# The MLP of an encoder layer: way up by Strassen's seven products, sums of the way down kept in DRAM

## The chip, the cores and the metric

The kernel runs on one core of a Trainium2 chip. The metric is device time in microseconds of one execution. The engines are named as in the profile: PE is TensorE's matmul, PEld its weight load, DVE VectorE, ACT ScalarE, POOL GpSimd, SP SyncE. POOL and SP do little but issue DMA transfers here.

## The reference, cut to what matters

Two layers of an encoder over 512 tokens of 1024 channels, all float32. Each has a mixer (three attentions, merged through gates) and an MLP with 4096 hidden channels; the change lies in the MLP.

```
for l in range(DEPTH):                       # DEPTH = 2
    h = _rmsnorm(x, g_mix[l])
    x = x + _mixer(h, ...)                   # ends with merged @ w_out
    h = _rmsnorm(x, g_mlp[l])
    x = x + jnp.square(jax.nn.relu(h @ w_up[l])) @ w_down[l]     # [512,1024] @ [1024,4096], [512,4096] @ [4096,1024]
return _rmsnorm(x, g_final)
```

## The kernel before, in words

Activations are kept transposed, channels on partitions: a chunk is 128 channels by 512 tokens. For precision every operand of a matmul is cut into a high and a low part (both float32r): a copy on ACT makes the high part, a subtraction on DVE the low one. A product is then three matmuls: high by high, high by low, low by high. `wblock` loads 512 KB of weights by a DMA on POOL's queue into a tile `raw` and cuts them into two tiles `w`; `mm3` runs the three matmuls for each of the chunks that it sums over.

**The order.** Nothing runs in the order of the code. `Plan` records all instructions, `schedule` lays them out by a planner's own costs on the five engines, with tiles from a common pool (`T` gives a tile by tag; at most 12 `w` and 6 `raw` live at a time, 8 banks of PSUM), and `emit` writes them out in that order, each engine's as one row. On the chip an engine then takes its instructions strictly in that order and waits by semaphores.

**The MLP.** The hidden channels are 16 pairs of chunks. The way up (`up_pair`) makes two chunks from the eight chunks of `h` by `mm3`: 48 matmuls of 512 columns a pair, then Relu and Square on ACT into a tile `hb`. The norm's factor is left out and multiplied in at the end (R2). The way down is done by Strassen's scheme in Winograd's form: a pair of chunks by two halves of the tokens (HB = 256) is a 2 by 2 block matrix, and so is the weight block, so seven products of 128 x 128 by 128 x 256 stand for eight. The halves' sums (`ht`) and their high and low parts (`u`) are made in `up_pair`, the weights' sums (`ss`) and parts (`w`) in `down_weights`. `PAIRS = (4, 4, 4)`: after each four pairs of the way up, `down` runs for each of the four pairs of output chunks (mp = 0 to 3), 7 x 4 x 3 = 84 matmuls of 256 columns, and `keep` takes the seven sums out of PSUM: copied by ACT into tiles `da` and `db` in the first group, added to them by DVE in the others. The last 4 of the 16 pairs go up and down in the plain way (8 chunks, `mm3`), and `outputs` puts the seven kept sums together on DVE beside that.

Before the MLP stands `wout`: for each of eight output chunks 24 matmuls, an addition to the residual stream `xt` on DVE, and `n2.chunk`, which scales the chunk by the norm's weights, cuts it in two parts (`h`) and sums its squares.

Of the kernel before, what the change touches and what calls it, by code (L numbers as in the profile page):

```python
# [11 lines left out]
F32 = mybir.dt.float32  # L12
# [8 lines left out]
S = 512  # L21
# [23 lines left out]
PAIRS = (4, 4, 4)  # L45
# [55 lines left out]
class Plan:  # L101
# [81 lines left out]
    def record(self, eng, m, args, kw):  # L183
# [8 lines left out]
        for v in outs:  # L192
            if isinstance(v, View):
                writes.append(v)
        for v in ins:
            if isinstance(v, View):
                reads.append(v)
# [416 lines left out]
def trunk(ctx, tc, x, w_in, b_gate, g_mix, diff_lambda, g_diff, g_cq, g_ckv, w_uq, w_ukv,  # L614
# [249 lines left out]
    def layer(l, norm):  # L864
# [714 lines left out]
        n2 = Norm(gmlp)  # L1579
        for mp in range(4):  # L1580
            for i in range(2):
                m = 2 * mp + i
                wh, wl = wblock(w_out[l], 0, 8, 128 * m)
                p = P("mm")
                mm3(p, wh, wl, merged)
                dve.tensor_add(xt[m], xt[m], p)
                n2.chunk(m, xt[m])
            dma(xs[mp], xm[mp])
# [6 lines left out]
        HB = S // 2  # L1595
        sums = {}

        def up_pair(c0):

            b = T("hb", [128, 2, 2, HB])  # L1600
            for i in range(2):
                wh, wl = wblock(w_up[l], 0, 8, c0 + 128 * i)
                p = P("mm")
                mm3(p, wh, wl, h)
                t = T("t")
                act.activation(t, p, AF.Relu)
                act.activation(b[:, i].rearrange("p t n -> p (t n)"), t, AF.Square)
            t13, t24 = T("ht", [128, 2, HB]), T("ht", [128, 2, HB])

            dve.tensor_sub(t13[:, 0], b[:, 0, 1], b[:, 0, 0])  # L1610
            dve.tensor_sub(t13[:, 1], b[:, 1, 1], b[:, 0, 1])
            dve.tensor_sub(t24[:, 0], b[:, 1, 1], t13[:, 0])
            dve.tensor_sub(t24[:, 1], t24[:, 0], b[:, 1, 0])
            parts = []
            for src in (b[:, :, 0], t13, t24):
                u = T("u", [128, 2, 2, HB], F32R)
                copy(u[:, 0], src)
                dve.tensor_sub(u[:, 1], src, u[:, 0])
                parts += [u[:, :, 0], u[:, :, 1]]
            if "u" not in sums:  # L1620
                sums["u"] = T("u", [128, 2, 2, HB], F32R)
                u = sums["u"][:, 0]
            else:
                u = sums.pop("u")[:, 1]
            hilo(u, b[:, 1, 1])
            b11, b21, t1, t3, t2, t4 = parts
            return [b11, b21, u, t4, t1, t2, t3]

        def down_weights(k0, n, mp):

            rows = w_down[l][128 * k0:128 * k0 + 256 * n, 256 * mp:256 * mp + 256].rearrange("(j i p) n -> p i j n", i=2, p=128)
            raw = [load(rows[:, i], n, 256).rearrange("p j (o n) -> p j o n", o=2) for i in range(2)]

            def four(t):
                return t[:, :256 * n].rearrange("p (a j n) -> p a j n", a=2, n=128)
            s12, s34 = four(T("ss", [128, 1024])), four(T("ss", [128, 1024]))

            dve.tensor_add(s12[:, 0], raw[0][:, :, 1], raw[1][:, :, 1])
            dve.tensor_sub(s12[:, 1], s12[:, 0], raw[0][:, :, 0])
            dve.tensor_sub(s34[:, 0], raw[0][:, :, 0], raw[0][:, :, 1])  # L1640
            dve.tensor_sub(s34[:, 1], raw[1][:, :, 0], s12[:, 1])
            wh, wl = pair()
            a1 = [four(w) for w in (wh, wl)]
            for i in range(2):
                copy(a1[0][:, i], raw[i][:, :, 0])
                dve.tensor_sub(a1[1][:, i], raw[i][:, :, 0], a1[0][:, i])
            a2 = four(T("w", [128, 1024], F32R))
            copy(a2[:, 0], raw[1][:, :, 1])
            dve.tensor_sub(a2[:, 1], raw[1][:, :, 1], a2[:, 0])
            ws = []  # L1650
            for s_ in (s12, s34):
                wh, wl = pair()
                copy(four(wh), s_)
                dve.tensor_sub(four(wl), s_, four(wh))
                ws += [(four(wh)[:, a], four(wl)[:, a]) for a in range(2)]
            s1, s2, s3, s4 = ws
            return [(a1[0][:, 0], a1[1][:, 0]), (a1[0][:, 1], a1[1][:, 1]), s4, (a2[:, 0], a2[:, 1]), s1, s2, s3]

        def product(o, n, ws, us):
            wh, wl = ws[n]  # L1660
            for j, u in enumerate(us):
                u0, u1 = u[n][:, 0], u[n][:, 1]
                ten.matmul(o, wh[:, j], u0, start=j == 0, stop=False)
                ten.matmul(o, wh[:, j], u1, start=False, stop=False)
                ten.matmul(o, wl[:, j], u0, start=False, stop=j == len(us) - 1)


        BANKS = ((0, 1), (5, 6), (3, 4), (2,))

        def down(k0, n, mp, us):  # L1670

            ws = down_weights(k0, n, mp)
# [8 lines left out]
        def keep(g, mp, pb):  # L1681

            if g == 0:
                t = T("da", [128, 2, 2, HB])
                if mp == 0:
                    sums["w"] = T("da", [128, 4, HB])
                sums[mp] = [t[:, 0], t[:, 1], T("db", [128, 2, HB]), sums["w"][:, mp]]
            for k in range(4):
                d, p = sums[mp][k], pb[k] if k < 3 else pb[k][:, 0]
                if g == 0:  # L1690
                    copy(d, p)
                else:
                    dve.tensor_add(d, d, p)

        def outputs(mp):

            c = T("hb", [128, 2, 2, HB])
            p12, p67, p45, p3 = sums[mp]
# [163 lines left out]
```

## Time and profile before

| | us |
|---|---|
| median of 3 runs (lowest to highest) | 1942.03 (1939.03 to 1942.73) |
| the profiled execution, its own time | 1941.78 |
| its span in the trace | 1940.0 |
| PE busy | 1910.4 (98%) |
| DVE busy | 1420.0 (73%) |
| ACT busy | 942.1 (49%) |
| POOL busy | 213.2 (11%) |

The MLP of layer 0 runs on PE from 630.91 to 973.85 us of the span, that of layer 1 from 1582.84 to about 1929, with stages of the same lengths. Matmuls are pipelined: the length that the profile gives for one is longer than its distance to the next, and the distance is read from the starts. The names in the trace are those of the tags; the banks of the Strassen products have the tag `x`. All instructions have line L600, that of the one call that issues them, so they are told apart by tile.

### The profile page before, as it was taken

The page shows a single profiled execution, that of the slowest core. Times are in us where ns is not written, and L with a number is a line of the kernel's source. Part 1 is how long each engine was busy: PE and PEld are TensorE (multiplying, and loading weights), DVE is VectorE, ACT ScalarE, POOL GpSimd, SP SyncE. Part 2 cuts the span into 40 slices and gives each one's busy share as a digit, 9 for nine tenths or more (in the row PEclk, how much of TensorE's full clock was granted, in tenths as well). Part 3 has the DMA queues.
Part 4 walks back from the last instruction along what each step waited for, and adds up shares of the span by engine and source line. Part 5 has one row for each costly group of instructions (what it writes and reads, how often), then busy time and mean ns, then how long its engine had stood idle before and what let it go on. Part 6 is the DMA issues. An engine that isn't in the chain of part 4 may idle for free.

```text
span 1940.0 us, 28120 instructions
## 1 busy us (share of the span) xinstructions
PE 1910.4 (98%) x10468; PEld 1634.1 (84%) x10468; DVE 1420.0 (73%) x3017; ACT 942.1 (49%) x1739; POOL 213.2 (11%) x260
## 2 busy tenths in 40 slices
PE   8999999999999999999999999999999999999998
PEld 7788888887878898998888888888877788898987
DVE  6788966787776656779557988677878766666874
ACT  5455644554344555444344755455434445545442
POOL 1000001100111020112100000011002111111200
PEclk9999999999999999999999999999999999999999
DMA  7954646577564241435357264365756542333521
GB/s 214 215 118 114 190 123 180 152 185 215 153 185 130 77 129 58 119 87 174 102 123 193 75 201 146 109 182 153 191 177 174 179 126 66 109 103 94 152 87 44
DMA packets 193825, 271.72 MB, mean 140 GB/s; under 512 B 98508, under 2 KB 129228, under 8 KB 193688
## 3 DMA queue, kind: packets, MB, share of 16 engines
q1 hardware_dynamic: 157368, 137.53, 25.7%
q0 software_dynamic: 36320, 132.40, 23.9%
q8 instruction: 82, 1.34, 0.3%
q14 instruction: 55, 0.45, 0.1%
HBM read 215.02 MB, written 50.67 MB: 137 GB/s over the span
## 4 chain that ended last, share of the span: by engine, by line
PE 88%; DVE 4%; DMA 4%; issue 3%; ACT 1%; SPq 0%; DVEq 0%; ACTq 0%; POOLq 0%
PE mm L600 65%; PE x L600 13%; PE s L600 4%; PE tp L600 3%; PE av L600 3%; DMA ml<-sm 1%; DVE sm L600 1%; DVE oo L600 1%; DMA sm<-ml 1%; DVE w L600 1%; DMA sm<-al 1%; DMA v<-in_x_dram 1%; DMA raw<-in_w_in_dram 1%; DVE pt L600 0%; DVE t L600 0%
## 5 line engine op out<-in xcount | busy, mean ns | idle before, releaser
L600 PE MATMUL mm<-h,w 128*128 128x512 f32 x3936 | 970.8, 397 | 0.2
L600 PEld LDWEIGHTS mm<-h,w 128*128 128x128 f32 x3936 | 728.4, 189 | 158.8 <-DVE w L600 1.0
L600 DVE TENSOR_TENSOR w<-raw,w 128x1024 fp32r<-128x1024 f32 (+3 forms) x390 | 361.7, 943 | 86.9 <-ACT w L600 73.7
L600 ACT ACTIVATE w<-raw 128x1024 fp32r<-128x1024 f32 (+3 forms) x390 | 314.0, 832 | 126.8 <-PE x L600 46.4
L600 PEld LDWEIGHTS x<-u,w 128*128 128x128 f32 x2016 | 239.6, 188 | 0.6
L600 PE MATMUL x<-u,w 128*128 128x256 f32 x2016 | 239.8, 281 | 0.0
L600 POOL DMA_DIRECT2D raw<-in_w_in_dram x86 | 74.8, 871 | 819.2 <-PE mm L600 259.3
L600 PE MATMUL mm<-w,h 128*128 128x256 f32 (+1 forms) x1152 | 157.3, 287 | 4.3 <-ACT h L600 1.7
L600 PEld LDWEIGHTS mm<-w,h 128*128 128x128 f32 x1152 | 150.4, 191 | 9.3 <-DVE w L600 2.2
L600 PE MATMUL s<-qk,qk 96*128 96x512 f32 (+2 forms) x448 | 122.5, 365 | 4.3 <-DVE sm L600 4.3
L600 ACT ACTIVATE p<-s,sm 128x512 f32<-128x512 f32 x128 | 87.5, 686 | 75.7 <-DVE sm L600 74.7
L600 DVE TENSOR_TENSOR t<-mm,const 128x512 f32<-128x512 f32 (+1 forms) x98 | 64.3, 675 | 72.0 <-PE mm L600 71.8
L600 PE MATMUL mm<-co,w 128*128 128x512 f32 x456 | 114.6, 398 | 0.1
L600 ACT ACTIVATE t<-mm 128x512 f32<-128x512 f32 x74 | 44.3, 598 | 143.7 <-PE mm L600 143.7
L600 ACT ACTIVATE pt<-tp 128x512 fp32r<-128x512 f32 x128 | 71.9, 596 | 82.9 <-PE tp L600 75.3
L600 PEld LDWEIGHTS mm<-co,w 128*128 128x128 f32 x456 | 84.7, 189 | 18.7 <-DVE co L600 0.5
L600 PE MATMUL mm<-om,w 128*128 128x512 f32 x384 | 98.7, 395 | 0.0
L600 PE MATMUL av<-pt,v 128*128 128x256 f32 x576 | 97.2, 290 | 1.3 <-DVE pt L600 1.2
L600 PEld LDWEIGHTS av<-pt,v 128*128 128x128 f32 x576 | 83.0, 188 | 15.5 <-DVE pt L600 4.1
L600 PEld LDWEIGHTS s<-qk,qk 128*128 128x128 f32 (+1 forms) x448 | 79.7, 188 | 19.0 <-DVE sm L600 5.5
L600 DVE TENSOR_REDUCE sm<-s 128x1 f32<-128x512 f32 x128 | 85.7, 682 | 12.2 <-PE s L600 11.8
L600 DVE TENSOR_TENSOR pt<-tp,pt 128x512 fp32r<-128x512 f32 x128 | 84.1, 683 | 8.7 <-ACT pt L600 8.1
(166 smaller groups left out, 2204.5 us busy)
## 6 DMA issues: line engine op xcount, KB each, us to landing
raw<-in_w_in_dram POOLq DMA_DIRECT2D x80, 512.0 KB, 7.0
raw<-in_w_up_dram POOLq DMA_DIRECT2D x64, 512.0 KB, 5.0
raw<-in_w_down_dram POOLq DMA_DIRECT2D x64, 512.0 KB, 4.9
dk<-rx SPq DMA_DIRECT2D x40, 512.0 KB, 5.6
qk<-dk SPq DMA_DIRECT2D x40, 512.0 KB, 5.4
raw<-in_w_in_dram SPq DMA_DIRECT2D x24, 512.0 KB, 9.0
dq<-rx SPq DMA_DIRECT2D x40, 256.0 KB, 3.9
qk<-dq SPq DMA_DIRECT2D x20, 512.0 KB, 3.9
```

The lines of the kernel that those rows point to most:

```text
L600: getattr(getattr(self.nc, op.eng), op.m)(*args, **kw)
```

## The change

- The way up of pairs 2 to 13 is done by seven products as well. The matrices are the eight chunks of the norm's input (4 pairs of chunks by 2 halves of the tokens) and blocks of `w_up`. `weights` replaces `down_weights` for both ways: it cuts seven blocks, each from `raw` or from a sum `ss`, into one tile `w` that holds both parts. The products of one call go to four banks and are put together on DVE and ACT between the products (`x`, `y`, `z`), before Relu and Square.
- The parts of the norm's input for this are made in the `wout` stage, by `n2_parts` and `halves`, in place of `n2.chunk`'s split into `h`. The pairs that go up in the plain way (0, 1, 14, 15) use the same parts, so their matmuls are halves of 256 columns, 96 a pair.
- `PAIRS = (4, 4, 3, 3)`: 14 pairs instead of 12 go down by seven products, in four groups instead of three. The last two pairs, 4 chunks, go down in the plain way.
- `keep` no longer holds the sums on the chip. ACT copies the seven products of each call from PSUM into two tiles `da` (1024 and 768 columns), and POOL issues one DMA for each to DRAM, a plain one in the first group, one that adds to what lies there (`accum_op`) in the others. `outputs` loads the sums back on SP's queue.

```diff
-PAIRS = (4, 4, 4)
+PAIRS = (4, 4, 3, 3)
+UP = frozenset(range(2, 14))
...
+        def n2_parts(mp):
+            b = T("hb", [128, 2, 2, HB])
+            for i in range(2):
+                copy(b[:, i].rearrange("p t n -> p (t n)"), xt[2 * mp + i], scale=gmlp[:, 2 * mp + i:2 * mp + i + 1])
+            return halves(b, len(UP) < 16)
...
+        def halves(b, both=False):
+            t13, t24 = T("ht", [128, 2, HB]), T("ht", [128, 2, HB])
+            dve.tensor_sub(t13[:, 0], b[:, 0, 1], b[:, 0, 0])
+            dve.tensor_sub(t13[:, 1], b[:, 1, 1], b[:, 0, 1])
+            dve.tensor_sub(t24[:, 0], b[:, 1, 1], t13[:, 0])
+            dve.tensor_sub(t24[:, 1], b[:, 1, 0], t24[:, 0])
+            parts = []
+            for src in (b[:, :, 0], t24, t13):
+                u = T("u", [128, 2, 2, HB], F32R)
+                copy(u[:, 0], src)
+                dve.tensor_sub(u[:, 1], src, u[:, 0])
+                parts += [u[:, :, 0], u[:, :, 1]]
+            u = shared("22")
+            hilo(u, b[:, 1, 1])
...
-                n2.chunk(m, xt[m])
+                n2.sq(xt[m])
+            hq2.append(n2_parts(mp))
...
-            s12, s34 = four(T("ss", [128, 1024])), four(T("ss", [128, 1024]))
...
+            def cut(src):
+                t = T("w", [128, 1024], F32R)[:, :256 * n].rearrange("p (a j n) -> p a j n", a=2, n=128)
+                copy(t[:, 0], src)
+                dve.tensor_sub(t[:, 1], src, t[:, 0])
+                return t[:, 0], t[:, 1]
+            def add(op, a, b):
+                t = T("ss", [128, 512])[:, :128 * n].rearrange("p (j n) -> p j n", n=128)
+                op(t, a, b)
+                return t
+            a11, a21, a12, a22 = (raw[i][:, :, o] for i in range(2) for o in range(2))
+            p1 = cut(a11)
+            s1 = add(dve.tensor_add, a21, a22)
+            s2 = add(dve.tensor_sub, s1, a11)
+            p6 = cut(s2)
+            p7 = cut(add(dve.tensor_sub, a11, a21))
+            p5 = cut(s1)
+            p2 = cut(a12)
+            p4 = cut(a22)
+            p3 = cut(add(dve.tensor_sub, a12, s2))
+            return [p1, p2, p3, p4, p5, p6, p7]
...
+            ws = weights(w_up[l], 0, 4, 256 * n)
+            pw, px, py, pz = (P("x0", [128, 2, HB]) for _ in range(4))
+            x, y, z = T("t"), T("ht", [128, 2, HB]), T("ht", [128, 2, HB])
+            product(pw[:, 0], 0, ws, hq2)
+            copy(x[:, :HB], pw[:, 0])
+            product(px[:, 1], 5, ws, hq2)
+            product(px[:, 0], 1, ws, hq2)
+            dve.tensor_add(y, px, x[:, :HB].unsqueeze(1).to_broadcast([128, 2, HB]))
+            act.activation(b[:, 0, 0], y[:, 0], AF.Relu)
+            product(py[:, 1], 6, ws, hq2)
+            product(py[:, 0], 4, ws, hq2)
+            copy(x[:, HB:], py[:, 0])
+            dve.tensor_add(z, py, y[:, 1:2].to_broadcast([128, 2, HB]))
+            dve.tensor_add(b[:, 1, 1], z[:, 1], x[:, HB:])
+            product(pz[:, 1], 3, ws, hq2)
+            product(pz[:, 0], 2, ws, hq2)
+            dve.tensor_add(flat[:, HB:3 * HB].rearrange("p (a n) -> p a n", a=2), z, pz)
+            act.activation(flat[:, HB:], flat[:, HB:], AF.Relu)
+            act.activation(flat, flat, AF.Square)
...
-                    dve.tensor_add(d, d, p)
+            t = T("da", [128, 4, HB]), T("da", [128, 4, HB])[:, :3]
             for k in range(4):
+                if k < 3:
+                    copy(t[k // 2][:, 2 * (k % 2):2 * (k % 2) + 2], pb[k])
+                else:
+                    copy(t[1][:, 2], pb[k][:, 0])
+            for d, x in zip(sums[mp], t):
+                x = x.rearrange("p a n -> p (a n)")
                 if g == 0:
-                    copy(d, p)
+                    plan.gpsimd.dma_start(d, x)
                 else:
+                    plan.gpsimd.dma_start(d, x, accum_op=OP.add)
...
+            a, b = T("da", [128, 4, HB]), T("da", [128, 4, HB])[:, :3]
+            for d, x in zip(sums[mp], (a, b)):
+                dma(x.rearrange("p a n -> p (a n)"), d)
```

Three places of the instructions' order show what this moves. The first is DVE in the way up of the second group of layer 0, one pair of chunks. In the names `w` is a part of weights, `ss` a sum of weights, `ht` a sum of halves, `u` a part of the activations, `hb` the pair itself. Before:

```order
L600 TENSOR_TENSOR w_7680<-raw_7533,w_7670 128x1024
L600 TENSOR_TENSOR ht_7651<-hb_7643 128x256
L600 TENSOR_TENSOR ht_7693<-hb_7643,ht_7651 128x256
L600 TENSOR_TENSOR ss_7698<-raw_7645 128x512
L600 TENSOR_TENSOR ht_7693<-ht_7693,hb_7643 128x256
L600 TENSOR_TENSOR u_7689<-hb_7643,u_7689 128x512
L600 TENSOR_TENSOR u_7695<-ht_7651,u_7695 128x512
L600 TENSOR_TENSOR u_7709<-ht_7693,u_7709 128x512
```

The same place now, where `x` is a bank of products:

```order
L603 TENSOR_TENSOR ht_8325<-x_1660_8249,t_8259 128x512
L603 TENSOR_TENSOR u_8320<-ht_8291,u_8320 128x512
L603 TENSOR_TENSOR w_8274<-raw_7988,w_8274 128x512
L603 TENSOR_TENSOR ht_8354<-x_1665_8288,ht_8325 128x512
L603 TENSOR_TENSOR w_8304<-ss_8127,w_8304 128x512
L603 TENSOR_TENSOR hb_8339<-ht_8354,t_8259 128x256
L603 TENSOR_TENSOR w_8313<-raw_8194,w_8313 128x512
L603 TENSOR_TENSOR hb_8339<-ht_8354,x_1673_8332 128x512
L603 TENSOR_TENSOR ss_8384<-raw_8194,raw_8210 128x512
```

Between the additions of products, each of which waits for PE, stand subtractions for the weights of later products.

The second is DVE beside the last, plain way down of layer 0, where `outputs` puts the sums together (`hb` from `da`), `const` is R2 and `xt` the residual stream. Before, it stands beside the last way up (`t` from `mm` is that way's square):

```order
L600 TENSOR_TENSOR xt_9176<-xt_9176,hb_9064 128x512
L600 TENSOR_TENSOR da_7276<-da_7276 128x256
L600 TENSOR_TENSOR hb_9299<-da_7392 128x256
L600 TENSOR_TENSOR da_7276<-da_7276,db_7337 128x256
L600 TENSOR_TENSOR hb_9084<-da_7276,db_7337 128x256
L600 TENSOR_TENSOR w_9310<-raw_9199,w_9295 128x1024
L600 SCALAR_TENSOR_TENSOR t_9306<-mm_9252,t_9306 128x512
```

Now it stands beside the way down itself (`t` from `mm` is a result of that way):

```order
L603 TENSOR_TENSOR hb_11129<-da_10947,da_10978 128x256
L603 TENSOR_TENSOR xt_10785<-xt_10785,hb_11129 128x512
L603 TENSOR_TENSOR hb_11129<-hb_11129,const_645 128x512
L603 TENSOR_TENSOR t_11173<-mm_11099,const_645 128x512
L603 TENSOR_TENSOR xt_10785<-xt_10785,hb_11129 128x512
L603 TENSOR_TENSOR xt_10744<-xt_10744,t_11173 128x512
L603 TENSOR_TENSOR t_11190<-mm_11112,const_645 128x512
L603 TENSOR_TENSOR w_11198<-raw_10997,w_11116 128x512
```

The last row makes the low part of weights that PE needs for the next products of the way down; ahead of it stand the sums and results.

The third is POOL's queue, from the way down to the next way up, in the first groups of layer 0. Before:

```order
L600 DMA raw_7992<-in_w_down_dram 128x4x256
L600 DMA raw_8003<-in_w_down_dram 128x4x256
L600 DMA raw_8063<-in_w_up_dram 128x8x128
L600 DMA raw_8092<-in_w_up_dram 128x8x128
L600 DMA raw_8182<-in_w_up_dram 128x8x128
```

Now, where `da_1024` and `da_768` on the left are sums in DRAM:

```order
L603 DMA raw_8586<-in_w_down_dram 128x4x256
L603 DMA raw_8613<-in_w_down_dram 128x4x256
L603 DMA raw_8645<-in_w_up_dram 128x4x256
L603 DMA da_1024_116<-da_8628 128x1024
L603 DMA da_768_117<-da_8654 128x768
L603 DMA raw_8718<-in_w_up_dram 128x4x256
L603 DMA da_1024_118<-da_8723 128x1024
```

The transfers of the sums stand between the weight loads of the next pairs.

## Rows read from the trace of the kernel before

**Rows 1.** The page's header: span, and busy time of each engine.

```profile
span 1940.0 us, 28120 instructions
PE 1910.4 (98%) x10468; PEld 1634.1 (84%) x10468; DVE 1420.0 (73%) x3017; ACT 942.1 (49%) x1739; POOL 213.2 (11%) x260
```

**Rows 2.** PE in order of time: start, length, tile and inputs, count [idle before].

```profile
760.68 39.88 PE L600 MATMUL x<-u,w 128*128 128x256 f32 x336
800.40 44.67 PE L600 MATMUL mm<-h,w 128*128 128x512 f32 x192
844.91 40.06 PE L600 MATMUL x<-u,w 128*128 128x256 f32 x336
884.81 44.61 PE L600 MATMUL mm<-h,w 128*128 128x512 f32 x192
```

**Rows 3.** Stages: length, busy PE, PEld, DVE, ACT, POOL, granted clock, DMA share, GB/s.

```profile
575.00:631.00 56.00, 56.00 (x244) 45.39 (x243) 36.69 (x50) 22.86 (x32) 8.57 (x10) 1.00 0.42 123
631.00:676.30 45.30, 45.30 (x199) 36.52 (x198) 32.13 (x66) 23.72 (x41) 4.49 (x6) 1.00 0.25 77
844.90:884.80 39.90, 39.90 (x337) 39.86 (x336) 36.00 (x57) 19.18 (x25) 8.57 (x10) 1.00 0.46 128
884.80:929.30 44.50, 44.50 (x195) 36.08 (x194) 37.39 (x61) 17.30 (x23) 7.81 (x9) 1.00 0.48 146
929.30:974.00 44.70, 44.70 (x195) 36.16 (x194) 26.45 (x36) 16.92 (x24) 5.91 (x7) 1.00 0.45 128
884.80:914.40 29.60, 29.60 (x130) 24.02 (x129) 29.56 (x52) 11.34 (x15) 6.18 (x7) 1.00 0.66 202
```

**Rows 4.** DVE in order of time, back to back: 512, 256 and 1024 elements.

```profile
888.67 0.68 DVE L600 TENSOR_TENSOR hb<-hb,const 128x512 f32<-128x512 f32 x1
889.27 0.42 DVE L600 TENSOR_TENSOR da<-da 128x256 f32<-128x256 f32 x1
889.60 0.68 DVE L600 TENSOR_TENSOR xt<-xt,hb 128x512 f32<-128x512 f32 x1
...
912.14 2.35 DVE L600 TENSOR_TENSOR w<-raw,w 128x1024 fp32r<-128x1024 f32 x2
914.41 0.68 DVE L600 SCALAR_TENSOR_TENSOR t<-mm,t 128x512 f32<-128x512 f32 x1
```

**Rows 5.** DVE: a result read by the next instruction.

```profile
852.28 0.68 DVE L600 TENSOR_TENSOR ss<-raw,raw 128x512 f32<-128x512 f32 x1
853.00 0.69 DVE L600 TENSOR_TENSOR ss<-ss,raw 128x512 f32<-128x512 f32 x1
```

**Rows 6.** ACT: two in a row; a group of the MLP (busy, mean ns).

```profile
853.58 1.16 ACT L600 ACTIVATE w<-raw 128x512 fp32r<-128x512 f32 x2 [3.87 <-PE x L600]
...
L600 ACT ACTIVATE w<-raw 128x1024 fp32r<-128x1024 f32 x35 | 36.1, 1051 | 11.0 <-PE mm L600 4.1 <-DMA raw<-in_w_up_dram 3.3 <-DVE w L600 1.8
```

**Rows 7.** DVE's waits in the MLP: for whom, us in total, times, longest.

```profile
DVE ht L600 <- ACT hb L600: 28.1, 11, 5.1
DVE w L600 <- ACT w L600: 20.8, 22, 3.8
```

**Rows 8.** ACT and DVE at the end of the third group's way up.

```profile
846.41 0.63 ACT L600 ACTIVATE u<-hb 128x512 fp32r<-128x512 f32 x1
846.41 0.42 DVE L600 TENSOR_TENSOR ht<-hb 128x256 f32<-128x256 f32 x1 [5.13 <-ACT hb L600]
```

**Rows 9.** DMA: POOL's issues, its queue (676 to 930 us), transfers to landing.

```profile
L600 POOL DMA_DIRECT2D raw<-in_w_up_dram x24 | 21.2, 885 | 80.8 <-DVE w L600 39.0 <-PE x L600 34.6 <-DVE da L600 7.1
q0 software_dynamic: 7009, 25.50, 35.0%
raw<-in_w_down_dram POOLq DMA_DIRECT2D x24, 512.0 KB, 5.1
dk<-rx SPq DMA_DIRECT2D x40, 512.0 KB, 5.6
xs<-xt SPq DMA_DIRECT2D x8, 512.0 KB, 2.9
```

More of the change, by code (lines that the diff above doesn't have):

```diff
@@ L194, in record @@
                 writes.append(v)
+        if kw.get("accum_op") is not None:
+            ins.append(args[0])
         for v in ins:
@@ L1592, in layer @@
         R2 = None
[L1595 to L1627, printed above, removed]
@@ L1660, in product @@
+        def product(o, n, ws, us, first=True, last=True):
             wh, wl = ws[n]
@@ L1662, in product, with up_pair @@
                 u0, u1 = u[n][:, 0], u[n][:, 1]
-                ten.matmul(o, wh[:, j], u0, start=j == 0, stop=False)
+                ten.matmul(o, wh[:, j], u0, start=first and j == 0, stop=False)
                 ten.matmul(o, wh[:, j], u1, start=False, stop=False)
-                ten.matmul(o, wl[:, j], u0, start=False, stop=j == len(us) - 1)
-        BANKS = ((0, 1), (5, 6), (3, 4), (2,))
+                ten.matmul(o, wl[:, j], u0, start=False, stop=last and j == len(us) - 1)
+        def up_pair(n):
+            b = T("hb", [128, 2, 2, HB])
+            flat = b.rearrange("p i t n -> p (i t n)")
+            if n not in UP:
+                for i in range(2):
+                    wh, wl = wblock(w_up[l], 0, 8, 256 * n + 128 * i)
+                    p = P("mm", [128, 2, HB])
+                    for t, ks in ((0, (0, 1)), (1, (7, 2))):
+                        mm3(p[:, t], wh, wl, [hq2[k // 2][ks[k % 2]] for k in range(KD)])
+                    act.activation(b[:, i], p, AF.Relu)
+                act.activation(flat, flat, AF.Square)
+                return b
+            ws = weights(w_up[l], 0, 4, 256 * n)
[16 more added lines that the diff above has]
+            act.activation(flat[:, HB:], flat[:, HB:], AF.Relu)
+            act.activation(flat, flat, AF.Square)
+            return b
+        BANKS = ((0, 5), (6, 4), (1, 3), (2,))
         def down(k0, n, mp, us):
-            ws = down_weights(k0, n, mp)
+            ws = weights(w_down[l], k0, n, 256 * mp)
             pb = []
@@ L1723, in layer @@
             for j in range(n):
-                us.append(up_pair(256 * (first + j)))
+                us.append(halves(up_pair(first + j)))
                 if g == 0 and j == 0:
@@ L1733, in layer @@
             first += n
-        us = [up_chunk(128 * c) for c in range(2 * first, 32)]
+        us = []
+        for n in range(first, 16):
+            b = up_pair(n)
+            for i in range(2):
+                u = H("u")
+                hilo(u, b[:, i].rearrange("p t n -> p (t n)"))
+                us.append(u)
         first *= 2
```

75 lines of the change are left out of this document (27 added, 48 removed).

## The prediction

> **What bounds the kernel now.** I read the page's header first, then TensorE (PE) in order of time through the MLP of layer 0, then the busy times of that stretch by stage, then VectorE (DVE) and ScalarE (ACT) instruction by instruction, and the DMA last. The header has PE busy 1910.4 of 1940.0 us, DVE 1420.0 and ACT 942.1 [rows 1]. In the MLP there is no gap at all on PE: the ways up and down follow each other with no idle time noted [rows 2], PE is busy for the whole of every stage, and its granted clock is 1.00, which is the 2.4 GHz level [rows 3]. So in the MLP the time is the number of matmuls times the distance from one start to the next, and a matmul that goes saves its distance, as long as the other engines keep up. They have room, but not everywhere: DVE is busy 26.45 of 44.70 us in the last way down, 37.39 of 44.50 in the last way up, 36.00 of 39.90 in the way down before it, and 29.56 of 29.60 where the results are put together [rows 3]. That last row shows that DVE can run without a gap.
>
> **The change part by part: PE.** Distances: 336 products of 256 columns take 39.72 and 39.90 us from their first start to the next stage's, 0.1185 us each; 192 of 512 columns take 44.51, 0.2318 each [rows 2]. A pair of hidden chunks that goes up by mm3 costs 48 x 0.2318 = 11.13 us, by seven products 7 x 4 x 3 = 84 x 0.1185 = 9.95. Twelve pairs of a layer change: 12 x 1.17 = 14.1 us saved. The four that stay plain now run as 96 halves: 11.38 us, 4 x 0.25 = 1.0 lost. On the way down pairs 12 and 13 go from 48 x 0.2318 to 4 x 21 x 0.1185: 2 x 1.17 = 2.3 saved. Together 15.4 us a layer, 30.8 in the kernel. (Counted over the whole program, PE gets 1368 more matmuls, nearly all of them of half the width.) This is the sure part; everything below is what is taken from it.
>
> **DVE.** From start to start DVE takes 0.60 us for 512 elements, 0.335 for 256 and 1.14 for 1024 [rows 4]; 384 lie between, some 0.47. One that reads the result just before it started 0.72 after it [rows 5]. ACT takes 0.53 for 512 [rows 6]. A Strassen pair of the way up needs on DVE 7 subs and 4 sums for the weights (11 x 0.604 = 6.64), three additions of products and a short one (2.15), and halves of the result (4 x 0.337 + 3 x 0.604 + 0.337 = 3.50): 12.3 us against PE's 9.95. A down call of four pairs needs 6.64 against 9.95, since keep now only copies, on ACT, and no longer adds on DVE; one of three pairs 11 x 0.47 = 5.2 against 63 x 0.1185 = 7.47. So the second group (4 up, 4 down) has 75.7 us of DVE for 79.6 of PE, the third and fourth (3 up, 4 down) 57.6 for 59.7: 95 to 96%, where the stages of before have 59 to 90% [rows 3]. The first has room: its two plain pairs cost DVE 5.8 each, 62.8 for 82.5. ACT, with some 8 us a pair and 5.4 a down call, has room everywhere.
>
> What the tight groups cost: in the ways up DVE falls behind by 4 x 2.34 = 9.4 us (second group) and 3 x 2.34 = 7.0 (third, fourth), and it can be ahead by about one call's weights, 6.6 us, since there are 12 tiles w at most and a call takes 7. That leaves 2.7 + 0.4 + 0.4 = 3.5 us a layer, 7 in all. Below, DVE never waits long enough to matter: 0. Above, it loses as much to waits as in the busiest way down, 3.9 of 39.9 us or 9.8% [rows 3], waits that mostly end with a result of ACT [rows 7]: 75.7 / 0.902 = 83.9 for 79.6, 57.6 / 0.902 = 63.9 for 59.7, 12.7 us a layer, 25 in all. I take 7, nearer the lower end, as the order of instructions mixes weights of other calls between the waiting ones, as it does in the stretch without gaps.
>
> **Ends of groups.** After the last up pair the first down call wants its parts. The chain is now an addition (0.68), Relu over 768 (between 0.63 for 512 and 1.05 for 1024, so 0.84), Square over 1024 (1.05), a copy (0.63) and hand-overs of some 0.35: 3.6 us to the first part, 4.3 to its low half [rows 4, 6, 8]. Before, a Relu and a Square of 512 took 846.41 - 844.91 = 1.5 us together, and PE did not idle [rows 2, 8]. PE has 33 (three pairs) or some 40 products that don't need the last pair, 3.9 to 4.7 us, and then a few more. I take 0.25 us at each of 8 ends, 2 in all, between 0 and 8.
>
> **Last way down.** It has only 45 us of PE (22.8 up, 22.3 down) for outputs of all four pairs of rows, which stood beside 44.5 + 44.7 before [rows 3]. From the DVE row that makes the low half of its first weight block to the one for its last there are 44 rows, 24.0 us by the distances above; PE has 19.6 us between its first uses of those two. The difference, 4.4, is what PE waits if DVE has no lead there; I take 2.5 in layer 0 and 1.5 in layer 1, where no parts for a next layer are made: 4, between 0 and 9.
>
> **Parts for the way up, made in wout.** DVE does 3.83 us for two chunks where it did 1.21, 10.5 us more a layer, ACT 8.8 more. DVE is idle 19.3 of 56.0 us in wout and 13.2 of the 45.3 after it [rows 3]; that hides it, and I cost it at nothing. Without the cover it would be at most 10 us a layer. Work before and after the MLP keeps its order on every engine.
>
> **DMA.** New are, in a layer, 32 transfers from SBUF to DRAM (24 of them adding), 14.7 MB, and 8 back, 3.7 MB. They are issued by POOL (some 0.9 us each [rows 9], POOL is busy 11% [rows 1]) and stand between the weight loads of the next calls, so a load behind one waits until ACT has copied the products. Loads took 25.5 MB for 35.0% of 254 us on 16 engines [rows 9], 3.49 us a MB. A group's weights are 8.4 MB (second) or 6.3 (third), 29.3 or 22.0 us; its sums are 3.67 MB, 12.8 us if adding costs as much as writing, and m times that otherwise. With m = 1 the DMA is 53% (second) and 58% (third) busy; with m = 2, 69 and 80%; with m = 3, 85 and 101%. No row shows an adding transfer. The nearest, plain writes of 512 KB, land after 2.9 us (xs) and 5.6 (dk), loads after some 5 [rows 9], so m = 1 is the lower end, at nothing lost. I take m = 2, a read and a write for each sum: nothing lost either, since weights are loaded ahead.
>
> The Trainium skill bears on m (DMA: Bandwidth & Descriptors, section Rules for kernel authors): an accumulating DMA reads its destination and writes it later. By that rule the bytes in DRAM double, which would speak for 2 and not for 1; no trace here shows it, and the sum is the same by either.
>
> **The sum.** The profiled execution took 1941.8 us, 1940.0 its span, and the median of the runs is 1942.0, so both are the same base. 1941.8 - 30.8 + 7 + 2 + 4 = 1924 us, 0.9% less. By the bounds of these costs it is 1911 to 1953.
>
> **The rivals.**
> A. The forecast, 1912 to 1937.
> B. DVE becomes the bound: the waits inside its chains cost it the 9.8%. For it: DVE at 95 to 96%, and every sub now waits for a copy on ACT and every pair for products. Against it: the gapless 29.6 us. 1941.8 - 30.8 + 25 + 2 + 4 = 1942; from an idle share of 5% on each further per cent costs some 5 us.
> C. Nothing is lost: PE stays gapless as it is in every stage before. 1911.
> D. Slower than before: adding in DRAM is so slow that DMA bounds the third and fourth groups. They fill all 16 engines at m = 2.95; beyond it two groups a layer grow by 12.8 us for each further 1.0 of m, so 51 us in the kernel. The gain of 18 is gone at m = 3.3, and with m = 4 the time is 1924 + 54 = 1978. For it: reading, adding and writing is more than writing, and POOL's loads queue behind. Against it: sums are not urgent, the weights have several free tiles, and the queue is idle most of the time now.
>
> That the change does not do what it says would be PE work that fails to fall; the counts of matmuls rule it out.
>
> **How the numbers follow.** A 0.60, C 0.09, B 0.17, D 0.14. Predicted is A's 1924. The range goes from C's 1911 to 1950, which takes in A, C and two thirds of B and leaves out D: 0.80. Faster by over 0.2% (below 1938, about what a measurement of this kernel can tell from no change): A, C and a fifth of B, 0.72. Within 0.2%: a good third of B and the mild end of D, 0.09. Slower: the rest, 0.19.
>
> **What would show it.** Right: PE busy some 31 us less; in the way up the rows of 256 columns 0.1185 us apart; DVE over 90% busy in the second to fourth groups; PE's idle time in the MLP 5 to 20 us in sum, released by DVE in the ways up and in the last way down. B: 30 us or more of PE idle released by DVE and ACT. D: PE, ACT or POOL waiting for transfers of weights, adding DMAs that land after 15 us or more, and a DMA share near 1. The prediction is wrong if products of 256 columns by seven tiles run slower than 0.1185, or if the first stage after wout waits for its parts.

## The result, and the profile after

The changed kernel took 1963.4 us (median of four runs, 1957.85 to 1965.78); the kernel before, on the same chip, 1940.8. The ratio of the runs is 1.0121, 95% interval 1.0104 to 1.0137 (the two medians alone give 1.0116): slower by 1.2%, where I had forecast 0.9% faster. The profiled execution took 1957.85 us. The columns below are those of [rows 1]; the last line is the share of the chain of waits that ended last.

```profile
span 1956.1 us, 32065 instructions
PE 1897.0 (97%) x11836; PEld 1685.8 (86%) x11836; DVE 1575.9 (81%) x3465; ACT 1081.6 (55%) x2139; POOL 269.4 (14%) x340
...
PE 61%; DVE 18%; issue 8%; DMA 8%; ACT 3%; POOL 1%; SPq 0%; ACTq 0%; POOLq 0%; DVEq 0%
```

PE has the 1368 matmuls more that were counted, and is busy 13 us less, in a span that is 16 us longer. In the MLP, where [rows 2] had no idle time at all, PE in order of time now reads like this (layer 0, from the second group's ways down to the last way down):

```profile
786.51 0.51 PE L603 MATMUL x<-u,w 128*128 128x256 f32 x2 [1.19 <-ACT w L603]
...
802.62 29.32 PE L603 MATMUL x<-u,w 128*128 128x256 f32 x246 [0.23 <-DVE w L603]
833.43 1.90 PE L603 MATMUL x<-u,w 128*128 128x256 f32 x13 [1.49 <-DVE w L603]
837.93 59.13 PE L603 MATMUL x<-u,w 128*128 128x256 f32 x491 [2.60 <-ACT u L603]
897.96 1.77 PE L603 MATMUL x<-u,w 128*128 128x256 f32 x12 [0.90 <-DVE w L603]
901.24 0.38 PE L603 MATMUL x<-u,w 128*128 128x256 f32 x1 [1.50 <-DVE w L603]
902.46 26.45 PE L603 MATMUL x<-u,w 128*128 128x256 f32 x219 [0.83 <-ACT u L603]
928.74 23.34 PE L603 MATMUL mm<-u,w 128*128 128x256 f32 x194
953.97 1.90 PE L603 MATMUL mm<-u,w 128*128 128x512 f32 x7 [1.90 <-DVE w L603]
958.32 12.72 PE L603 MATMUL mm<-u,w 128*128 128x512 f32 x47 [2.46 <-DVE w L603]
```

Three places lose time: the ways down of the second group (after its first call; one of its waits ends at 786 us), the first call after a group's way up (833 to 838, 898 to 902), and the last way down (954 to 958). To put numbers on it I took, for each stage, the time from its first matmul to the next stage's and subtracted the count of its matmuls times 0.1185 or 0.2318 us, the distances of [rows 2]. This is what the stages of layer 0 lost, in the kernel after and in those of the experiments below (us; where a kernel has three groups, the lines run over three):

| | after | plain writes | no adding | less DVE | 3 groups | planner, 4 groups | planner, 3 groups | no way up | sums on chip |
|---|---|---|---|---|---|---|---|---|---|
| ways up after the first group's | 1.2 | -0.2 | -0.2 | 1.0 | 0.8 | 3.5 | -0.1 | -0.3 | 10.5 |
| first call of each way down | 11.8 | 7.2 | 2.8 | 6.3 | 9.4 | 6.1 | 4.2 | -0.1 | 11.9 |
| its other calls | 3.9 | 0.1 | 0.1 | 4.1 | 15.1 | 0.2 | 0.1 | -0.3 | 3.5 |
| last way down | 7.8 | 2.7 | 2.7 | 7.9 | 0.0 | 4.9 | 0.0 | 0.1 | 0.0 |
| sum | 24.7 | 9.8 | 5.4 | 19.3 | 25.3 | 14.7 | 4.2 | -0.6 | 25.9 |

Layer 1 of the kernel after lost about 25 us: 2.3, 13.8 and 4.4 in the first three lines, and in its last way down 4.9 more than the 2.9 that this stage loses by the same measure in the kernel before, where the last matmuls stand between others. The two layers make some 50 us. The sure part of the forecast, 1941.8 - 30.8 = 1911, lies 46.9 below the profiled execution; the stretches outside the MLP are some 4 us shorter than before (1.5 ahead of the first MLP, 2.6 between the two). So PE's saving is there, and these stages hold the whole difference.

**How one such loss comes about.** Four engines in order of time, in the second group's ways down:

```profile
780.87 0.85 POOL L603 DMA_DIRECT2D da<-da  x1 [4.16 <-ACT da L603]
...
785.83 0.63 ACT L603 ACTIVATE w<-raw 128x512 fp32r<-128x512 f32 x1 [3.73 <-DMA da<-da]
...
786.50 0.69 DVE L603 TENSOR_TENSOR w<-raw,w 128x512 fp32r<-128x512 f32 x1 [2.46 <-ACT w L603]
...
786.51 0.51 PE L603 MATMUL x<-u,w 128*128 128x256 f32 x2 [1.19 <-ACT w L603]
```

POOL issues an adding transfer at 780.87. ACT stands from 782 to 785.83 for its landing, 4.9 us after the issue, although it only wants to copy weights from `raw` to `w`. The transfer goes to DRAM, which ACT doesn't read; so what ACT waits for is the tile that it is to write, the one from which the transfer reads. DVE waits behind ACT, PE behind both. In the whole program (waits by engine: for whom, us in total, times, longest; in the last line DVE waits for sums that are loaded back):

```profile
DVE w L603 <- ACT w L603: 100.9, 77, 6.3
ACT w L603 <- DMA da<-da: 42.2, 22, 4.1
DVE hb L603 <- DMA da<-da: 21.4, 2, 11.6
```

**How it reaches the ends of groups.** Stages of layer 0 (columns as in [rows 3]): the second group's ways down, the third group's ways up without their first calls, the start of its ways down, the fourth group's sums with the last ways up, and the last way down until PE runs again:

```profile
753.30:798.20 44.90, 41.95 (x338) 40.29 (x337) 33.41 (x58) 22.20 (x40) 12.13 (x15) 1.00 0.67 145
802.60:829.40 26.80, 26.77 (x226) 26.78 (x227) 26.73 (x52) 19.93 (x42) 5.50 (x7) 1.00 0.50 124
829.40:837.90 8.50, 4.44 (x35) 3.99 (x33) 8.50 (x19) 5.30 (x11) 0.76 (x1) 1.00 0.04 5
907.70:951.40 43.70, 43.70 (x371) 43.70 (x370) 25.81 (x50) 21.64 (x41) 13.41 (x16) 1.00 1.02 289
959.10:963.40 4.30, 4.30 (x13) 3.37 (x12) 4.30 (x11) 0.63 (x1) 1.33 (x2) 0.60 0.52 161
```

DVE stood idle 11.5 of 44.9 us in the ways down (6.5 of 41.8 with plain writes, 3.4 of 41.6 without adding transfers, in the experiments below), then ran 26.73 of 26.80 and 8.50 of 8.50 us without a gap. It entered the ways up with no lead, needs 12.3 us a pair there for PE's 9.95 by the prediction's count, and was late when the last pair came. In DVE's and ACT's rows at the end of that group:

```profile
832.82 0.55 DVE L603 TENSOR_TENSOR w<-ss,w 128x384 fp32r<-128x384 f32 x1
833.29 0.42 DVE L603 TENSOR_TENSOR hb<-ht,t 128x256 f32<-128x256 f32 x1
833.62 0.56 DVE L603 TENSOR_TENSOR w<-raw,w 128x384 fp32r<-128x384 f32 x1
834.09 0.56 DVE L603 TENSOR_TENSOR w<-ss,w 128x384 fp32r<-128x384 f32 x1
834.56 0.69 DVE L603 TENSOR_TENSOR hb<-ht,x 128x512 f32<-128x512 f32 x1
...
835.28 1.93 ACT L603 ACTIVATE hb<-hb 128x768 f32<-128x768 f32 x2 [2.85 <-DVE hb L603]
```

PE began the first product of the way down at 829.40, so the last pair's products were through by then; DVE added them (`hb` from `ht` and `x`) at 834.56, 5.2 us later. The chain behind it ran as predicted (834.56 to 837.93, 3.4 us).

**The last way down.** From 907.7 to 951.4 the 16 DMA engines are full (1.02): the fourth group's adding transfers, the last ways' weights, the residual stream and the loading back of the sums fall together. Adding transfers issued there land after 7.8 to 13.1 us. DVE waits 11.6 us for sums, and then does the outputs of which the prediction spoke, while PE waits for weights (the two waits at 954 and 958 above):

```profile
946.94 1.10 DVE L603 TENSOR_TENSOR hb<-da,da 128x256 f32<-128x256 f32 x3 [11.56 <-DMA da<-da]
```

The last row of the stages above shows one more price of such waits. Behind the second of them PE's granted clock was 0.60 on average for 4.3 us, which cost 1.6 us by itself. In layer 1 the same happened three times, at the ends of the third and fourth groups and in the last way down; a stretch of 3.4 us at 0.50 costs some 1.7. So an estimated 6 to 7 of the 50 us lost are not waits but the slower clock after them:

```profile
1795.60:1799.00 3.40, 2.96 (x14) 2.96 (x15) 3.40 (x9) 2.28 (x5) 0.00 (x0) 0.51 0.32 116
1863.90:1867.30 3.40, 3.40 (x19) 3.40 (x18) 3.40 (x8) 1.83 (x4) 0.91 (x1) 0.50 0.00 0
1918.50:1921.90 3.40, 2.96 (x7) 2.38 (x8) 3.40 (x8) 0.27 (x1) 0.75 (x1) 0.50 0.25 77
```

### The profile page after: what moved, and what is told of

Its sections match the earlier page's. It is cut to its first block, busy times and chain, and to the rows that moved or that the text cites. A ratio compares the mean times of both kernels' runs of the same rounds, so it can differ in the third digit from the quotient of the medians.

```text
span 1956.1 us, 32065 instructions
## 1 busy us (share of the span) xinstructions
PE 1897.0 (97%) x11836; PEld 1685.8 (86%) x11836; DVE 1575.9 (81%) x3465; ACT 1081.6 (55%) x2139; POOL 269.4 (14%) x340
## 3 DMA queue, kind: packets, MB, share of 16 engines
HBM read 222.36 MB, written 80.03 MB: 155 GB/s over the span
## 4 chain that ended last, share of the span: by engine, by line
PE 61%; DVE 18%; issue 8%; DMA 8%; ACT 3%; POOL 1%; SPq 0%; ACTq 0%; POOLq 0%; DVEq 0%
PE mm L603 45%; PE x L603 6%; DVE w L603 6%; PE s L603 4%; PE tp L603 3%; DMA da<-da 3%; PE av L603 3%; DVE ht L603 3%; DVE ss L603 2%; DVE hb L603 2%; DVE u L603 2%; DVE sm L603 1%; DMA ml<-sm 1%; ACT w L603 1%; POOL da L603 1%
## 5 line engine op out<-in xcount | busy, mean ns | idle before, releaser
L603 PE MATMUL mm<-h,w 128*128 128x512 f32 x2400 | 610.6, 398 | 0.2
L603 PE MATMUL x<-u,w 128*128 128x256 f32 x4368 | 533.0, 283 | 23.0 <-DVE w L603 11.3
L603 PEld LDWEIGHTS x<-u,w 128*128 128x128 f32 x4368 | 524.0, 190 | 31.5 <-DVE w L603 15.4
L603 PEld LDWEIGHTS mm<-h,w 128*128 128x128 f32 x2400 | 439.5, 189 | 90.6 <-DVE w L603 1.0
L603 DVE TENSOR_TENSOR w<-raw,w 128x512 fp32r<-128x512 f32 (+4 forms) x438 | 355.3, 825 | 69.6 <-ACT w L603 67.8
L603 ACT ACTIVATE w<-raw 128x512 fp32r<-128x512 f32 (+4 forms) x438 | 311.5, 736 | 87.8 <-DMA raw<-in_w_in_dram 29.0
L603 DVE TENSOR_TENSOR w<-ss,w 128x512 fp32r<-128x512 f32 (+1 forms) x224 | 141.6, 653 | 33.8 <-ACT w L603 33.0
L603 PE MATMUL mm<-u,w 128*128 128x256 f32 (+1 forms) x984 | 141.4, 304 | 8.0 <-DVE w L603 8.0
L603 ACT ACTIVATE w<-ss 128x512 fp32r<-128x512 f32 (+1 forms) x224 | 127.6, 595 | 37.1 <-DMA da<-da 18.5
L603 PEld LDWEIGHTS mm<-u,w 128*128 128x128 f32 x984 | 130.4, 191 | 18.5 <-DVE w L603 10.4
```

What stands on the lines that cost most here:

```text
L603: getattr(getattr(self.nc, op.eng), op.m)(*args, **kw)
```

## The experiments

The theory, T: an adding transfer holds the tile that it reads longer than the order allows for; ACT and DVE wait for the tile, DVE loses its lead, and, being some 95% loaded, doesn't get it back before the end of the group. The rival, V: DVE has too much to do in the ways up, whatever the transfers do. A third, M: the price of adding on the DMA engines is the loss itself. The kernel before took 1935.0 us on the chip of the first three experiments and of the one with three groups, 1936.7 on that of the parts alone and of the planner's two costs raised together, 1935.0 on that of the landing raised alone and of one pair more, so ratios to it are compared; the kernel after stands at 1.0121.

### Plain writes in place of adding ones

```diff
             kw = {k: self.real(v) for k, v in op.kw.items()}
+            kw.pop("accum_op", None)
```

> The changed kernel with its instructions in the same order on every engine; the 48 adding transfers of the sums write instead of adding (the sums of the earlier groups are therefore left out of the result). Theory T (transfers): the order gives a transfer of sums some 3 us to land, as the plain ones of the first group do (2.6 to 6.0 us), but the adding ones took 4.6 to 13.1 us; the tiles they read come free late, ACT's copies of weights wait for those tiles, DVE loses its lead in the ways down of the second to fourth groups, and shows it at the ends of groups and in the last way down. By T plain writes land in 3 to 6 us and the time falls by 30 to 45 us, to 1915 to 1930. Rival V (VectorE): DVE has too much work in the ways up (12.3 us a pair beside 9.95 of PE) whatever the transfers do; the time stays within 8 us, 1950 to 1965.

Measured 1919.0 us, ratio 0.9917 (0.9900 to 0.9933), in T's range and far below V's: 39 us below the kernel after at its ratio on this chip (1.0121 x 1935.0 = 1958.4). The order is the same; what changed is the transfers, their landing and their issue (some 0.55 us on POOL for 0.86). Transfers of sums (size of one, median us from issue to landing, the plain ones of the first group among them), first in the kernel after, then in this one:

```profile
da<-da POOLq DMA_DIRECT2D x32, 512.0 KB, 6.2
...
da<-da POOLq DMA_DIRECT2D x32, 384.0 KB, 6.2
```

```profile
da<-da POOLq DMA_DIRECT2D x32, 512.0 KB, 4.8
da<-da POOLq DMA_DIRECT2D x32, 384.0 KB, 5.2
```

The second group's ways down and the third's ways up read here (columns as above):

```profile
752.00:793.80 41.80, 40.68 (x338) 40.01 (x337) 35.35 (x61) 25.21 (x46) 10.13 (x16) 1.00 0.54 176
793.80:823.60 29.80, 29.80 (x254) 29.80 (x253) 29.58 (x58) 22.62 (x48) 5.60 (x8) 1.00 0.34 117
```

In the ways up DVE is just as full (29.58 of 29.80), and PE loses nothing: a full DVE is no loss here as long as it starts ahead. V is out as the whole cause. It keeps a part: the third group's first call lost 4.2 us in layer 0 here too, with DVE without a gap. A wait for ACT, which waits for DVE, is 2.3 of them; most of the rest is again the clock behind the wait:

```profile
830.00:835.00 5.00, 4.96 (x28) 4.96 (x29) 5.00 (x12) 2.08 (x4) 1.21 (x2) 0.66 0.31 102
```

### No adding transfers

```diff
-            getattr(getattr(self.nc, op.eng), op.m)(*args, **kw)
+            if "accum_op" not in kw:
+                getattr(getattr(self.nc, op.eng), op.m)(*args, **kw)
```

> The changed kernel in the same order, without the 48 adding transfers (the copies into their tiles stay; the result lacks the sums of all groups but the first). T: like the run with plain writes or up to 5 us less, 1912 to 1930, since POOL's queue and the DMA engines are free as well. If the plain writes leave the time and this one lowers it by over 15 us, it is POOL's issue time and the queue and not the adding. V: within 8 us of the changed kernel.

Measured 1910.5, ratio 0.9872 (0.9856 to 0.9888), 8.5 us below the plain writes, a little below T's range. So of 48 us that the adding transfers cost, 39 are the adding, and 9 belong to transfers as such. POOL's issue time is not the main thing: taking away all 48 issues with their transfers gains less than a quarter of what the plain writes gain.

These three runs also give the price of adding. The queue of POOL, over the whole program (packets, MB, share of 16 engines), in the kernel after, with plain writes, and without:

```profile
q0 software_dynamic: 45280, 161.76, 30.4%
```

```profile
q0 software_dynamic: 43744, 161.76, 27.0%
```

```profile
q0 software_dynamic: 38368, 139.74, 23.9%
```

Shares times spans (1956.1, 1915.6, 1911.2) are 594.7, 517.2 and 456.8 us. If all other transfers on the queue cost the same in the three kernels, the 22.0 MB cost 60.4 us written and 137.9 added: adding takes 2.28 times as long as writing.

### Less work on DVE, adding as it was

In the ways up `skip` is true for the blocks p7, p5, p4 and p3. When the planned order is written out, a subtraction with `skip` is left out, and a matmul with `high` takes that operand.

```diff
-                dve.tensor_sub(t[:, 1], src, t[:, 0])
+                dve.tensor_sub(t[:, 1], src, t[:, 0]).skip = skip
...
-                ten.matmul(o, wl[:, j], u0, start=False, stop=last and j == len(us) - 1)
+                op = ten.matmul(o, wl[:, j], u0, start=False, stop=last and j == len(us) - 1)
+                op.high = wh[:, j] if skip else None
```

> The changed kernel in the same order with its adding transfers, but four of the seven low parts of weights in each pair of the way up by seven products are not made on DVE (96 subtractions of 512 elements in all; TensorE takes the high part in their place, with as many matmuls), so DVE needs 9.9 us a pair in place of 12.3. V: the ends of the second to fourth groups lose under 1 us each in place of 4 to 6, and the time falls by 20 us or more, to 1940 or less. T: the losses in the ways down stay (some 5 us a layer), and only what DVE can catch up goes, 8 to 15 us: 1943 to 1952.

Measured 1943.7, ratio 1.0043 (1.0029 to 1.0057): 14.7 us less than after, inside T's range and above V's. The other calls of the ways down still lose 4.1 us in layer 0 and the last way down 7.9; the third group's first call loses 3.8 (5.0 before this edit), the fourth's 1.4 (4.2). ACT waits for transfers as long as in the kernel after:

```profile
ACT w L607 <- DMA da<-da: 40.3, 21, 3.8
```

So at the ends of groups both play a part: late tiles take DVE's lead, and a full DVE doesn't win it back. The losses inside the ways down and in the last way down stay with this edit, which relieves DVE in the ways up alone.

### One part alone: sums in DRAM, plain way up

```diff
-PAIRS = (4, 4, 3, 3)
-UP = frozenset(range(2, 14))
+PAIRS = (4, 4, 4)
+UP = frozenset()
```

> One part alone: the sums of the way down go to DRAM by adding transfers, with three groups of four pairs as before, but all pairs go up in the plain way (by halves of 256 columns, 96 a pair in place of 48 of 512: 4 us a layer more on PE than before). The planner's costs are those of the changed kernel. DVE has room now (5.8 us a pair of the way up for 11.4 of PE). T: the adding transfers still hold tiles too long, but DVE catches up, so the ways down lose under 4 us a layer: 1938 to 1950, and the ends of groups lose under 1 us each. If the adding itself costs as much as in the run with three groups of four pairs and the way up by seven products (losses of some 20 us a layer), 1965 to 1985.

Measured 1942.6, ratio 1.0036 (1.0025 to 1.0047), in T's range. PE has 8 us more than before by its matmuls, and 5.9 is the difference. Nothing is lost in any stage, though the DMA is as busy as in the kernel after (two stages, second group's way up and down):

```profile
715.10:760.50 45.40, 45.40 (x387) 45.40 (x386) 28.45 (x50) 21.77 (x37) 8.35 (x11) 1.00 0.38 125
760.50:800.10 39.60, 39.60 (x339) 39.60 (x338) 22.89 (x35) 25.45 (x43) 11.72 (x13) 1.00 0.73 155
```

With DVE at 28 of 45 and 23 of 40 us adding transfers cost nothing (32 of them, in another order). That speaks against M.

### The other part alone: Strassen's way up, sums on the chip

```diff
-PAIRS = (4, 4, 3, 3)
+PAIRS = (4, 4, 4)
...
+            for k in range(4):
+                d, p = sums[mp][k], pb[k] if k < 3 else pb[k][:, 0]
+                if g == 0:
+                    copy(d, p)
+                else:
+                    dve.tensor_add(d, d, p)
```

> The other part alone: the way up of pairs 2 to 13 by seven products, the sums kept on the chip and added by DVE, and three groups of four pairs, all as before the change. No transfers of sums. DVE's work for a group of four pairs up and four calls down is then 84 us (12.3 a pair, 6.6 + 2.1 a call) for 79.6 of PE, and 9 tiles more are taken. T and V agree that DVE is the bound here: 4 to 10 us lost in each of the second and third groups, 1940 to 1960. If the way up alone loses nothing (its DVE work is hidden), 1916 to 1922.

Measured 1960.9, ratio 1.0125 (1.0110 to 1.0140), just above the range. Here DVE is the bound by itself (ways up of the second and third groups):

```profile
712.90:755.90 43.00, 40.48 (x339) 39.87 (x338) 42.98 (x80) 30.87 (x59) 3.00 (x4) 1.00 0.23 77
...
801.80:847.20 45.40, 41.33 (x339) 40.04 (x338) 45.40 (x85) 31.80 (x61) 2.98 (x4) 1.00 0.25 81
```

In this form the way up by seven products needs the sums off DVE; the change was right to pair the two.

### One part undone: three groups

```diff
-PAIRS = (4, 4, 3, 3)
+PAIRS = (4, 4, 4)
```

> One part undone: three groups of four pairs as before (PAIRS 4, 4, 4), so the last way down has 8 chunks again and there is one group less of adding transfers (32 in place of 48); the way up by seven products for pairs 2 to 13 and the sums in DRAM stay. PE's work rises by 2.3 us a layer, 4.7 in all. T: the adding transfers lose what they lose a group, so a third of the loss goes and the last way down has room for its outputs: 1925 to 1945. If the last way down and the fourth group cost nothing (their losses are only moved), 1955 to 1968.

Measured 1954.5, ratio 1.0099 (1.0083 to 1.0116), a miss for T's number, and half a us below the range given for losses that are only moved: the last way down of layer 0 loses nothing any more, but the third group's ways down lose 11 us more, and ACT waits for transfers longer than before:

```profile
ACT w L603 <- DMA da<-da: 62.5, 26, 8.8
```

A third fewer adding transfers didn't take a third of the loss away. The number of transfers doesn't decide it; where the order puts them, and for which tile they are late, is what T leaves, and the next runs test that.

### An order made for the longer landing

The planner takes an adding transfer for a plain write. In the first kernel both its time on the DMA engines and its landing were raised, in the second the landing alone, in the third both, with three groups. Nothing else changes; no work is added or taken.

```diff
             self.more = 1100 if out else 2000
+            if kw.get("accum_op") is not None:
+                lat *= 1.6
+                self.more += 1500
```

> The changed kernel with one cost of its planner altered: an adding transfer is planned with 1.6 times the time on the DMA engines and 1.5 us more to landing, near what the trace shows, so the order keeps its tile longer and puts other work between. Nothing else changes; as many transfers, as much work on PE, DVE and ACT. Theory T (tiles that come free late): ACT waits for transfers of sums under 15 us in the whole kernel in place of 42, the ways down lose less, and the time falls by 15 to 35 us, to 1925 to 1945. If only the price of adding on the DMA engines counts and not the order (rival M), the stretch with the loads, the adding and the loading back stays full, and the time falls by under 10 us. Theory V (DVE has too much work): no change, within 8 us.

> The changed kernel with four groups; the planner takes an adding transfer to land 3 us later than it did, and leaves its time on the DMA engines as it was, so only the tiles are held longer in the plan, and the spacing of transfers is planned as before. Theory T1 (late tiles alone): as with both costs altered, 1925 to 1938. Theory T2 (the queue: loads of weights planned behind adding transfers that take longer than planned): the first adding transfers of each group still come too close, and a good part of the loss stays, 1940 to 1955.

(its edit is `self.more += 3000` without the factor)

> The same altered planner cost, and three groups of four pairs (PAIRS 4, 4, 4), so 32 adding transfers in place of 48 and a last way down of 8 chunks that hides the outputs. By T both losses go, and what is left is the gain on PE less some us: 1905 to 1922, faster than the kernel before by 0.7 to 1.6%. By M (price of adding) the transfers still fill the third group: 1925 to 1945. By V DVE's load in the second and third groups stays and their ends lose 4 to 6 us each: 1935 to 1950.

Measured 1932.3, 1931.6 and 1916.0 us; ratios 0.9981 (0.9972 to 0.9991), 0.9981 (0.9969 to 0.9994) and 0.9894 (0.9878 to 0.9911). T's ranges for the time hold all three. In the first kernel the four groups' other calls lose 0.2 us instead of 3.9, and ACT waits 16.1 us for transfers, a little over the 15 that were expected:

```profile
ACT w L606 <- DMA da<-da: 16.1, 15, 2.5
```

and the transfers land later than in the kernel after:

```profile
da<-da POOLq DMA_DIRECT2D x32, 512.0 KB, 8.1
da<-da POOLq DMA_DIRECT2D x32, 384.0 KB, 7.8
```

They take 8.1 and 7.8 us where they took 6.2, and the kernel is 27 us faster (0.9981 for 1.0121): what counts is not how long they take but whether the order knows it. That rules M out for the ways down. The landing alone did as well, outside the range of the second kernel's T2. But only the calls behind the first are clean in its trace (0.1 us lost in layer 0): in its profiled execution, the longest of ten at 1938.5 us, the first calls still lost 10.2 and the last way down 10.8 in layer 0, so for these the trace doesn't settle T1 against T2. What stays with four groups in the first kernel is the first calls (6.1) and the last ways up and down (3.5 and 4.9), where the DMA is nearly full (0.89 in the last ways up); three groups remove the latter, at a DMA share of 0.91 in the last ways up. One rival is left untested: each raised cost gives a wholly new order, and no run raised another cost by as much, so how much a new order alone would move the time is not shown. Three settings that raise an adding transfer's landing gained, and none lost. PE in the third kernel:

```profile
757.43 79.04 PE L606 MATMUL x<-u,w 128*128 128x256 f32 x660 [0.20 <-ACT u L606]
836.73 1.32 PE L606 MATMUL x<-u,w 128*128 128x256 f32 x9 [0.27 <-DVE w L606]
838.54 56.75 PE L606 MATMUL x<-u,w 128*128 128x256 f32 x475 [0.49 <-DVE w L606]
895.12 67.41 PE L606 MATMUL mm<-u,w 128*128 128x256 f32 x384
```

It beats the kernel before by 1.1%, and the kernel after by 2.2%.

### One pair more

```diff
-UP = frozenset(range(2, 14))
+UP = frozenset(range(2, 15))
...
+                lat *= 1.8
+                self.more += 1000
```

> The best version so far (three groups of four pairs, adding transfers planned at a longer time) with one pair more, 14, going up by seven products, and 1.8 times and 1.0 us for 1.6 times and 1.5 us. PE has 1.4 us a layer less to do, 2.8 in the kernel; DVE has 6.5 us more in the last way up, where it puts the outputs together. If DVE has that room: 1911 to 1915. If not, it loses what it wins or more: 1915 to 1925.

Measured 1918.6, ratio 0.9909 (0.9892 to 0.9926), not told apart from 0.9894 and in the range that was given for a DVE without room: what PE saves, the last way down (1.2 us in layer 0 for 0.0) and the third group's first call (2.2 for 1.6) take.

An experiment that gives the sums tiles of their own, the most direct test of T, was not tried.

## Why the prediction was wrong, step by step

**PE, right.** A way up of four pairs takes 39.7 us (713.57 to 753.31) for 336 products, 0.1183 each, and a plain pair in halves 11.35 us. With plain writes PE's busy time is 1882.2 us, 28 less than before (31 predicted), and without adding transfers 24.5 of the 30.8 us arrive in the time; in the kernel after, busy time includes matmuls that were slowed between waits.

**DVE and the ends of groups, right in size for a kernel with plain writes, in part by luck.** 7 + 2 us were predicted for both; with plain writes these stages and the other calls lost 7.2 us in layer 0 and 1.9 in layer 1, where the prediction had the layers alike. And it is not lost where I put it: the ways up lose nothing, and DVE's lag comes out at the first call of the way down, where nothing hides the chain from the last pair. Some 1.7 us of the 7.2 are the clock, which the prediction didn't count. In the kernel after the same stages lost 16.9 in layer 0.

**Last way down.** 2.5 was predicted for layer 0, 2.7 came with plain writes, 7.8 with adding. For layer 1, 1.5 was predicted; 0.7 more than in the kernel before came with plain writes, 4.9 more with adding.

**Parts in wout, right.** The MLP starts at 629.43 (630.91 in [rows 2]'s kernel), and its first stage has no idle time.

**DMA: the step that failed.** It reads "I take m = 2 ...: nothing lost either, since weights are loaded ahead". The price was near enough, and rather too high: the prediction's m multiplies the price of the loads, 3.49 us a MB, and adding took 137.9 us for 22.0 MB, 6.27 a MB, so m is 1.80 in these terms (a plain write took 2.74, so 2.28 times that). The second group as a whole, from 713.6 to 798.2, shows a DMA share of 0.53 for the 69% given, its ways down alone 0.67. The Trainium skill (DMA: Bandwidth & Descriptors, section Rules for kernel authors) has an accumulating DMA read its destination and write it later; the time agrees with that, 2.28 times a plain write's, though no row shows the reading itself. The conclusion, nothing lost, was wrong: the adding cost 39 us by the run with plain writes. I asked whether the transfers fit on the engines and whether weights come in time. I did not ask how long the tile under a transfer is held, and who is given it next. The waits show it: ACT, which "has room everywhere" by its busy time, stood 42.2 us in the kernel for tiles under transfers, and DVE, behind it, 11.5 of 44.9 us in the second group's ways down of layer 0. And I priced DVE and DMA as independent terms, though at the ends of groups DVE at 95% was just what made the late tiles expensive.

**The rivals.** D had the sign and the cause, adding transfers, but not the mechanism: it let them decide only from m = 2.95, by filling the engines. At the measured price, 1.80 in its terms, they fill them in one stretch (1.02 from 907.7 to 951.4), because I had counted the sums beside their own group's weights and not beside the residual stream and the sums that are loaded back. B had the right signs in the profile, DVE over 90% in the ways up and PE released by DVE and ACT, but took its 9.8% of idle time from waits inside DVE's chains. The idle time was 26% (11.5 of 44.9), in the ways down, and its root was a transfer.

What is not settled: why the third group's first call waits 2.3 us in layer 0 with plain writes (and pays for it again by the clock) and loses only 0.5 in layer 1, with DVE without a gap in both.

## What to carry to other kernels

A transfer out of a tile costs three things: its time on the DMA engines, its issue, and the tile until it lands; look for who writes that tile next. An engine at 95% hides little: a wait that it made up here at 60% came back as lost time at the next place where nothing hid its chain. Where a plan fixes the order, measure a new kind of transfer first and teach its landing to the plan: that was worth 27 us here, nearly the change's own saving.

## What the runs showed of the hardware

- An adding transfer to DRAM cost 2.28 times a plain write's time on the DMA engines. In the second group, same order, adding ones landed after 4.7 to 8.1 us (median 5.4), plain ones after 2.6 to 7.2 (median 3.9). POOL's issue took some 0.86 us for an adding one and 0.55 for a plain one.
- The profile's count of bytes read from HBM is 222.36 MB in all three of these kernels: if adding reads its destination, the count doesn't show it.
- After PE stood idle 1.90 and 2.46 us shortly one after the other in the last way down, its granted clock was 0.60 on average from 959.1 to 963.4, so at the 1.2 GHz level for most of it: eight matmuls of 512 columns came 0.2 us late each, 1.6 us on top of the waits. After 1.49 and 2.60 us at the end of the third group of layer 0 it stayed at 1.00; after 1.39 and 2.61 at the same place of layer 1 it was 0.51 from 1795.6 to 1799.0. With plain writes it was 0.66 on average from 830 to 835 after a single wait of 2.31 us. In the MLP before, without idle time, it was 1.00 throughout [rows 3].
